# A sample's cached keys: rewritten in memory in blocks of 32, and turned by VectorE instead of TensorE

## The chip, the cores and the metric

The kernel runs on one core of a Trainium2 chip. The metric is the device time of one execution in microseconds; the kernel before took 1939.15 us (median of 3 runs, 1937.5 to 1939.77). The engines of the core work side by side, each in the order of its own instruction list: TensorE (PE: matmuls and transposes by matmul, with its weight loads PEld), VectorE (DVE), ScalarE (ACT), GpSimd (POOL) and SyncE (SP). All DMAs of this kernel are issued from SP's list.

## The reference

One step of a one-layer hybrid trunk, in float32: a normalization, one input projection to 5648 columns, three groups (RG-LRU, dilated-window attention, Mamba-2 SSD), gates, one output projection and a second normalization. There is a prompt of 2048 tokens and there are 8 samples of 4 tokens, each sample with a cache of 1024 positions of keys and values, 8 heads of 64. The change concerns the samples' attention:

```python
DILATIONS = ((128, 1), (512, 4), (2048, 16))

def band_attn_sample(q, k_all, v_all, W, slopes, window, dil):
    span = window // dil
    jd = jnp.arange(span + 1) * dil
    idx = W + jnp.arange(L)[:, None] - jd[None, :]
    ...
    kg = k_all[:, idx]
    vg = v_all[:, idx]
    s = jnp.einsum('blhd,bljhd->blhj', q, kg, preferred_element_type=f32) * (Dh ** -0.5)
    s = s - slopes[:, None] * jd.astype(f32)
    ...
    o = jnp.einsum('blhj,bljhd->blhd', p.astype(vg.dtype), vg, preferred_element_type=f32) / l[..., None]
```

With a cache of 1024 positions the three windows of a sample's 4 tokens reach the last 512 cached positions and, in the first 512, those of the first four residues of every 16: 128 positions. So 640 cached keys of each head are scored.

## The kernel before

The program is written as Python generators that are run in turn; the framework's scheduler then fixes each engine's list and puts in the waits. Where several instructions could go next, the list by and large follows the order in which the program creates them. Each engine, SP too, works through its list strictly in order: an instruction that waits holds all behind it.

**Input projections.** `load_w(c0)` (L140 on) loads a weight tile of 1024x128: SP issues the DMA into `wr` (L143, one buffer), POOL multiplies by the norm's gain (L146), ScalarE makes the rounded part `wh` (L147), VectorE the remainder `wl` (L148); `wh` and `wl` have two buffers each. `project_steps` (L154 on) runs five chunks of tokens over it, each with 8 x 3 matmuls (`mm3`, L82 to L84: `wh` by `xh`, `wh` by `xl`, `wl` by `xh`), then evacuates the chunk and gives one turn to every generator in the list `behind`:

```python
            evac(ps, t0, n)
            for g in behind:
                next(g, None)
            yield
```

The order of the early projections is: values and dt for all tokens (`project_tokens`), then `q_tile(0)`, `q_tile(1)`, `lru_x(0)`, `q_tile(2)`, `ga_tile(0)`, `lru_g(0)`, `lru_x(1)`, `q_tile(3)` and so on. `q_tile`, `ga_tile` and `lru_g` store each evacuated chunk by DMA (`d_q`, `d_ga`, `d_y`). `lru_x(m)` also loads eight small blocks `wab` (L525), and its rest (convolution, gates, then a tail with the scan at L582) runs in turns beside the two projections that follow.

**The samples' attention** (`sample_part`, L887 on) is done for 4 pairs of heads and 2 groups of 4 samples, eight parts in turn, with the steps of seven projections `z_tile` between them. A part loads its keys in two pieces of 2 samples (`kc`, `load_rows`, L879) and one of the far positions (`kf`, `load_far`, L885), turns them by five groups of four TensorE transposes (L903) into PSUM, and copies them into `ktT` (head dimension by 640 positions for 4 samples), with ScalarE and VectorE taking the copies alternately (`evac_copy`). Then come the scores (L924), the softmax on VectorE and ScalarE, six transposes of the weights (L946), the product with the values (L958) and the combination of the two heads.

Of the kernel before, what the change touches and what calls it, by code (L numbers as in the profile page):

```python
# [8 lines left out]
F32 = mybir.dt.float32  # L9
# [23 lines left out]
def tile_hybrid_step(ctx: ExitStack, tc: tile.TileContext, A):  # L33
    nc = tc.nc
    act, dve, pool, pe, sp = nc.scalar, nc.vector, nc.gpsimd, nc.tensor, nc.sync
# [5 lines left out]
    dram = ctx.enter_context(tc.tile_pool(name="dram", bufs=1, space=DRAM))  # L41
# [9 lines left out]
    d_ys = dram.tile([1024, NS], F32, name="d_ys")  # L51
    d_cums = dram.tile([16, NS], F32, name="d_cums")
    d_z = dram.tile([1024, TOK], F32, name="d_z")


    ident = const.tile([128, 128], F32, name="ident")
# [73 lines left out]
    psT = ps_es.enter_context(tc.tile_pool(name="psT", bufs=2, space=PSUM, side="right"))  # L130
# [22 lines left out]
    behind = []  # L153
# [163 lines left out]
    with tc.tile_pool(name="rows", bufs=1) as rp:  # L317
# [10 lines left out]
        tp = psT.tile([128, 4, 128], F32, tag="tp", name="tp")  # L328
# [3 lines left out]
        for g in range(3):  # L332
            tp = psT.tile([128, 4, 128], F32, tag="tp", name="tp")
# [5 lines left out]
        tp = psT.tile([128, 4, 128], F32, tag="tp", name="tp")  # L339
# [6 lines left out]
        dve.tensor_scalar(out=sp8[:, 0], in0=sp8[:, 0], scalar1=-8.0, scalar2=None, op0=OP.mult)  # L346


    def by_residue(ap, np_):

        return ap[:, :np_].rearrange("p (n i r) -> p n r i", r=4, i=32)
# [37 lines left out]
    def k_tile(m):  # L389
        rows = slice(128 * m, 128 * m + 128)  # L390
        k_p = A["k_p"][0, 0].rearrange("t h d -> t (h d)")

        def evac(ps, t0, n):
            np_ = min(n, SEQ - t0)
            kr = p2.tile([128, 512], F32, tag="e", name="kr")
            dve.tensor_copy(out=blocks(kr, np_), in_=by_residue(ps, np_))
            sp.dma_start(out=d_k[rows, t0:t0 + np_], in_=kr[:, :np_])

            ko = p2.tile([128, 512], F32, tag="e", name="ko")
            dve.transpose(out=ko[:, :n], in_=ps[:, :n])  # L400
            for a in range(4):
                pt_, fs = slice(32 * a, 32 * a + 32), slice(128 * m + 32 * a, 128 * m + 32 * a + 32)
                sp.dma_start(out=k_p[t0:t0 + np_, fs].rearrange("(b i) f -> i b f", i=32),
                             in_=ko[pt_, :np_].rearrange("i (b f) -> i b f", f=32))
                if n > np_:
                    sp.dma_start(out=A["k_s"][0].rearrange("b l h d -> (b l) (h d)")[:, fs], in_=ko[pt_, np_:n])
            if n > np_:
                act.copy(out=ksn[:, m], in_=ps[:, np_:n])
        project(C_K + 128 * m, evac)
# [101 lines left out]
    with tc.tile_pool(name="lru", bufs=1) as lp, tc.tile_pool(name="lrus", bufs=2) as ls:  # L511
# [99 lines left out]
        tp = psT.tile([128, 4, 128], F32, tag="tp", name="tp")  # L611
# [6 lines left out]
        sp.dma_start(out=A["lru_h_s"][0], in_=lo[28:36])  # L618

    p2_es.close()  # L620


    z_last = []
# [8 lines left out]
    with tc.tile_pool(name="xbc", bufs=2) as xp, tc.tile_pool(name="xbc1", bufs=1) as xp1:  # L632
        scol = xp1.tile([128, 12, 27], F32, name="scol")
        for m in range(12):
# [4 lines left out]
            for t0, n in CHUNKS:  # L639
                o = xp.tile([128, 512], F32, tag="o", name="o", bufs=3)  # L640
# [3 lines left out]
        for g in range(3):  # L644
            so = xp.tile([27, 512], F32, tag="o", name="so", bufs=3)
            tp = psT.tile([128, 4, 128], F32, tag="tp", name="tp")
# [214 lines left out]
    with tc.tile_pool(name="sa", bufs=1) as sa:  # L861
        evac_n = [0]

        def evac_copy(out, in_):
            evac_n[0] += 1
            if evac_n[0] % 2:
                act.copy(out=out, in_=in_)
            else:
                dve.tensor_copy(out=out, in_=in_)
# [5 lines left out]
        def load_rows(t, cache, pr, bg, b0):  # L875

            rows = cache[0, 4 * bg + b0:4 * bg + b0 + 2].rearrange("b t h d -> b t (h d)")[:, :, 128 * pr:128 * pr + 128]
            for i in range(2):
                sp.dma_start(out=t[:, i], in_=rows[i, 512:1024].rearrange("(j p) c -> p j c", p=128))  # L879

        def load_far(t, cache, pr, bg):

            rows = cache[0, 4 * bg:4 * bg + 4].rearrange("b t h d -> b t (h d)")[:, 0:512, 128 * pr:128 * pr + 128]
            for m in range(4):
                sp.dma_start(out=t[32 * m:32 * m + 32], in_=rows.rearrange("b (g s) c -> s g b c", s=16)[m])  # L885

        def sample_part(pr, bg):  # L887
# [2 lines left out]
            sbias = sa.tile([128, 672], F32, tag="sbias", name="sbias")  # L890
            sp.dma_start(out=sbias, in_=A["c_sbias"][pr, bg])
            ktT = sa.tile([128, 4, 640], F32, tag="ktT", name="ktT")
            for i in range(3):
                if i < 2:
                    kt_ = sa.tile([128, 2, 4, 128], F32, tag="kc", name="kc", bufs=2)
                    load_rows(kt_, A["cache_attn_k"], pr, bg, 2 * i)
                else:
                    kt_ = sa.tile([128, 1, 4, 128], F32, tag="kf", name="kf")
                    load_far(kt_[:, 0], A["cache_attn_k"], pr, bg)
                for h in range(2 if i < 2 else 1):  # L900
                    tp = psT.tile([128, 4, 128], F32, tag="tp", name="tp")
                    for j in range(4):
                        pe.transpose(tp[:, j], kt_[:, h, j], ident)  # L903
                    if i < 2:
                        evac_copy(ktT[:, 2 * i + h, :512], tp.rearrange("p j c -> p (j c)"))
                    else:
                        evac_copy(ktT[:, :, 512:], tp)
                    yield
            for i in range(2):
                load_rows(vt[i], A["cache_attn_v"], pr, bg, 2 * i)  # L910
            load_far(vf, A["cache_attn_v"], pr, bg)
# [3 lines left out]
            for e in range(2):  # L915
                pt_ = slice(64 * e, 64 * e + 64)
                pool.tensor_copy(out=qz[pt_, :, 4 * e:4 * e + 4],
                                 in_=qs[pt_, pr, 16 * bg:16 * bg + 16].rearrange("p (b l) -> p b l", l=NL))
# [8 lines left out]
            p = sa.tile([128, 672], F32, tag="p", name="p")  # L927
# [13 lines left out]
            for g in range(2):  # L941
                tp = psT.tile([128, 4, 128], F32, tag="tp", name="tp")
# [10 lines left out]
            o = psG.tile([128, 512], F32, tag="g", name="so")[:, :128]  # L953
# [10 lines left out]
            tp = psT.tile([128, 4, 128], F32, tag="tp", name="tp")  # L964
# [9 lines left out]
        def fills():  # L974

            parts = [sample_part(pr, bg) for pr in range(4) for bg in range(2)]
            for i, part in enumerate(parts):
                for j in range(6):
                    next(part)
                    yield  # L980
                    if i and j < 4:
                        next(parts[i - 1])
                        yield
            for _ in parts[-1]:
                yield
# [412 lines left out]
    psT = es.enter_context(tc.tile_pool(name="psT2", bufs=1, space=PSUM, side="right"))  # L1398
# [123 lines left out]
    for c in range(16):  # L1522
        k = 0
# [115 lines left out]
```

## Time and profile before

| what | value |
|---|---|
| median of 3 runs | 1939.15 us |
| the profiled execution's own time | 1935.46 us |
| its span | 1933.7 us |
| TensorE busy | 1888.0 us, 98% |
| VectorE, ScalarE, POOL busy | 1075.8, 760.3, 269.4 us |
| mean share of the 16 DMA engines (SP's queue) | 38.7% |

How to read it: the profile is of one execution, and its rows are compared with that execution's own time; the other runs lie up to 4.3 us above it. Busy time is the time in which an engine executes something; matmuls are pipelined, and their ends are modelled, so neighbours overlap and the spacing of their starts tells the cost. Rows of SP (SPq) are the issuing of a DMA, not its transfer. In brackets stands how long the engine was idle ahead of an instruction and which instruction of which engine ended that.

### The profile page before, as it was taken

The numbers are of one execution on the slowest core, as the hardware profiler recorded it, in microseconds if no ns is written. First come the engines' busy times: TensorE is split into PE (matmuls) and PEld (weight loads), VectorE is DVE, ScalarE is ACT, GpSimd is POOL, SyncE is SP. The second block draws the span as 40 slices with busy tenths as digits, with TensorE's granted clock in tenths as the row PEclk, the third lists the DMA queues.
The fourth block names the chain that finished last, engine by engine and source line by source line (L and its number), as shares of the span: only waits on it lengthen the run. The fifth ranks groups of instructions, "written<-read, shape, count | busy, mean of one in ns | idle before, by whom it ended". The sixth has DMA issues, their size and how long they took to land.

```text
span 1933.7 us, 35729 instructions
## 1 busy us (share of the span) xinstructions
PE 1888.0 (98%) x14110; PEld 1552.6 (80%) x14110; DVE 1075.8 (56%) x2354; ACT 760.3 (39%) x1490; POOL 269.4 (14%) x346
## 2 busy tenths in 40 slices
PE   8999999999999999999999999999998999999998
PEld 7998888888888888887877777777766787677876
DVE  7414444454533776664422226666687776667774
ACT  6411636362610222223233436555654333333332
POOL 0100111101010111111000100000023223223231
PEclk9999999999999999998999999999999999999999
DMA  7422121232233222224477753343465444334442
GB/s 235 131 79 74 44 69 47 64 69 63 66 88 79 94 76 74 67 72 138 131 210 205 208 181 115 101 142 102 119 207 161 127 140 124 111 115 130 128 140 66
DMA packets 304500, 222.02 MB, mean 115 GB/s; under 512 B 69171, under 2 KB 260515, under 8 KB 304333
## 3 DMA queue, kind: packets, MB, share of 16 engines
q1 hardware_dynamic: 304332, 219.74, 38.7%
q8 instruction: 111, 1.82, 0.4%
q14 instruction: 57, 0.46, 0.1%
HBM read 150.81 MB, written 68.86 MB: 114 GB/s over the span
## 4 chain that ended last, share of the span: by engine, by line
PE 41%; ACT 4%; DMA 3%; DVE 3%; issue 1%; SPq 1%; POOL 1%; DVEq 0%; ACTq 0%; POOLq 0%
PE ops L83 5%; PE ops L84 5%; PE ops L82 5%; PE mm L82 3%; PE pt L1164 3%; PE mm L84 3%; PE mm L83 3%; PE o L1200 2%; ACT sr L1136 2%; PE s L1109 2%; PE yd L1283 2%; DMA sg<-d_cum 1%; PE yo L1288 1%; PE s L1088 1%; PE stp L1307 1%
## 5 line engine op out<-in xcount | busy, mean ns | idle before, releaser
L82 PE MATMUL mm<-xh,wh 128*128 128x512 f32 (+2 forms) x1600 | 562.4, 351 | 1.8 <-ACT wh L147 0.9
L83 PE MATMUL mm<-xl,wh 128*128 128x512 f32 (+2 forms) x1600 | 561.2, 351 | 0.0
L84 PE MATMUL mm<-xh,wl 128*128 128x512 f32 (+2 forms) x1600 | 559.9, 350 | 0.0
L82 PEld LDWEIGHTS mm<-xh,wh 128*128 128x128 f32 x1600 | 301.5, 188 | 44.4 <-issue 4.3
L84 PEld LDWEIGHTS mm<-xh,wl 128*128 128x128 f32 x1600 | 300.6, 188 | 39.6 <-issue 1.0
L83 PEld LDWEIGHTS mm<-xl,wh 128*128 128x128 f32 x1600 | 301.2, 188 | 37.7 <-issue 0.2
L146 POOL TENSOR_TENSOR wr<-wr,gC 128x1024 f32<-128x1024 f32 x40 | 78.7, 1968 | 407.6 <-DMA wr<-in_w_in_dram 379.5
L436 DVE SCALAR_TENSOR_TENSOR o<-u,ssdc,o 128x512 f32<-128x512 f32 (+2 forms) x216 | 128.6, 618 | 4.8
L1136 ACT ACTIVATE sr<-sr,nm 128x384 f32<-128x384 f32 (+3 forms) x128 | 97.9, 770 | 23.3 <-DVE nm L1132 18.7
L148 DVE SCALAR_TENSOR_TENSOR wl<-wr,wh 128x1024 fp32r<-128x1024 f32 x40 | 48.9, 1223 | 82.9 <-ACT wh L147 82.9
L642 ACT ACTIVATE o<-o 128x512 f32<-128x512 f32 (+2 forms) x60 | 33.1, 552 | 145.7 <-issue 83.2
L1047 ACT COPY ptsb<-pt 128x512 f32<-128x512 f32 x96 | 52.5, 583 | 76.7 <-PE pt L1164 76.6
L720 DVE TENSOR_SCALAR sg<-sg,cum 128x128 f32<-128x128 f32 (+1 forms) x256 | 72.8, 344 | 14.7 <-ACT ecB L718 14.6
L82 PE MATMUL mmt<-wh,xh 128*128 128x256 f32 (+3 forms) x272 | 79.5, 295 | 0.9 <-ACT xh L254 0.6
L84 PE MATMUL mmt<-wh,xl 128*128 128x256 f32 (+3 forms) x272 | 78.6, 290 | 0.0
L83 PE MATMUL mmt<-wl,xh 128*128 128x256 f32 (+3 forms) x272 | 78.1, 288 | 0.0
L434 DVE TENSOR_SCALAR o<-u,ssdc 128x512 f32<-128x512 f32 (+1 forms) x72 | 43.1, 611 | 61.9 <-ACT u L416 60.7
L1164 PE MATMUL pt<-ident,sr 128*128 128x128 f32 x576 | 75.3, 281 | 2.3 <-ACT sr L1136 1.8
L147 ACT ACTIVATE wh<-wr 128x1024 fp32r<-128x1024 f32 x40 | 42.4, 1060 | 87.9 <-PE mm L83 76.9
L1164 PEld LDWEIGHTS pt<-ident,sr 128*128 128x128 f32 x576 | 63.6, 143 | 15.0 <-issue 8.9
L416 ACT COPY u<-mm 128x512 f32<-128x512 f32 (+1 forms) x80 | 39.4, 493 | 91.9 <-PE mm L84 80.2
L718 ACT ACTIVATE ecB<-sg 64x512 f32<-64x512 f32 x60 | 37.8, 630 | 88.3 <-DMA sg<-d_cum 80.5
(520 smaller groups left out, 3551.3 us busy)
## 6 DMA issues: line engine op xcount, KB each, us to landing
wr<-in_w_in_dram SPq DMA_DIRECT2D x40, 512.0 KB
sg<-d_cum SPq DMA_DIRECT2D x30, 512.0 KB
d_xbc<-o SPq DMA_DIRECT2D x36, 256.0 KB
x<-in_x_prompt_dram SPq DMA_DIRECT2D x32, 256.0 KB
kc<-in_cache_attn_k_dram SPq DMA_DIRECT2D x32, 256.0 KB
vt<-in_cache_attn_v_dram SPq DMA_DIRECT2D x32, 256.0 KB
xres<-in_x_prompt_dram SPq DMA_DIRECT2D x32, 256.0 KB
out_dram<-ot SPq DMA_DIRECT2D x32, 256.0 KB
```

Of the source, the lines that this page charges most:

```text
L82: pe.matmul(out, lhsT=wh, rhs=xh, start=start, stop=False)
L83: pe.matmul(out, lhsT=wh, rhs=xl, start=False, stop=False)
L84: pe.matmul(out, lhsT=wl, rhs=xh, start=False, stop=stop)
L146: pool.tensor_tensor(out=wr, in0=wr, in1=gC[:, :, None].to_broadcast([128, 8, 128]), op=OP.mult)
L147: act.activation(out=wh, in_=wr, func=AF.Copy, scale=scale)
L148: dve.scalar_tensor_tensor(out=wl, in0=wr, scalar=scale, in1=wh.bitcast(F32), op0=OP.mult, op1=OP.subtract)
L434: dve.tensor_scalar(out=o, in0=v(0), scalar1=w[:, 0:1], scalar2=b, op0=OP.mult, op1=OP.add)
L436: dve.scalar_tensor_tensor(out=o, in0=v(t), scalar=w[:, t:t + 1], in1=o, op0=OP.mult, op1=OP.add)
L720: dve.tensor_scalar(out=sg[:n, h], in0=sg[:n, h], scalar1=cum[:n, c, 8 * g + h:8 * g + h + 1], scalar2=0.0, op0=OP.subtract, op1=OP.min)
L1047: act.copy(out=out, in_=in_)
L1136: act.activation(out=sr[e][r], in_=sr[e][r], func=AF.Exp, bias=nm[:, e, r:r + 1], accum_out=ll[:, e, r:r + 1])
L1164: pe.transpose(tp[:, r], sr[e][r][:, 128 * g:128 * g + 128], ident)
```

## The change

A tile in memory, `d_kc`, takes the 640 reachable keys of every sample, cut so that each 32x32 block of a position block by head dimension lies where VectorE's transpose of 32x32 blocks needs it. `spread_keys` fills it with DMAs from memory to memory: 8 DMAs for each of 32 blocks, one with 512 pieces of 128 bytes and one with 128 such pieces for each of four samples. The generator `key_blocks` stands in `behind` before `q_tile(0)`, so one block is issued in the program at each of the first 32 projection steps, up to the second of `lru_x(1)`. In `sample_part` four loads of 128x640 take the place of the eight loads of keys, and four `dve.transpose` of 128x640 that of the 20 transposes on TensorE and the five copies from PSUM. `evac_copy` is now called once in a part, for the softmax weights, so ScalarE and VectorE take that copy in turns. All lines behind the new ones move on by one at first and by 18 or 19 later (L147 becomes L148).

```diff
--- before.py
+++ after.py
@@ -51,6 +51,7 @@
     d_ys = dram.tile([1024, NS], F32, name="d_ys")
     d_cums = dram.tile([16, NS], F32, name="d_cums")
     d_z = dram.tile([1024, TOK], F32, name="d_z")
+    d_kc = dram.tile([1024, 4 * 640], F32, name="d_kc")
 
 
     ident = const.tile([128, 128], F32, name="ident")
@@ -346,6 +347,23 @@
         dve.tensor_scalar(out=sp8[:, 0], in0=sp8[:, 0], scalar1=-8.0, scalar2=None, op0=OP.mult)
 
 
+    def spread_keys(pr, bg):
+
+        rows = A["cache_attn_k"][0, 4 * bg:4 * bg + 4].rearrange("b t h d -> b t (h d)")
+        for a in range(4):
+            o = 128 * (2 * pr + bg) + 32 * a
+            fs = slice(128 * pr + 32 * a, 128 * pr + 32 * a + 32)
+            dst = d_kc[o:o + 32].rearrange("k (b t f) -> k b t f", b=4, f=32)
+            for b in range(4):
+                sp.dma_start(out=dst[:, b, :16], in_=rows[b, 512:1024, fs].rearrange("(t k) f -> k t f", k=32))
+
+                sp.dma_start(out=dst[:, b, 16:], in_=rows[b, 0:512, fs].rearrange("(k t) f -> k t f", t=16)[:, :4])
+            yield
+
+    key_blocks = (None for pr in range(4) for bg in range(2) for _ in spread_keys(pr, bg))
+    behind.append(key_blocks)
+
+
     def by_residue(ap, np_):
 
         return ap[:, :np_].rearrange("p (n i r) -> p n r i", r=4, i=32)
@@ -618,6 +636,9 @@
         sp.dma_start(out=A["lru_h_s"][0], in_=lo[28:36])
 
     p2_es.close()
+    behind.remove(key_blocks)
+    for _ in key_blocks:
+        pass
 
 
     z_last = []
@@ -890,22 +911,14 @@
             sbias = sa.tile([128, 672], F32, tag="sbias", name="sbias")
             sp.dma_start(out=sbias, in_=A["c_sbias"][pr, bg])
             ktT = sa.tile([128, 4, 640], F32, tag="ktT", name="ktT")
-            for i in range(3):
-                if i < 2:
-                    kt_ = sa.tile([128, 2, 4, 128], F32, tag="kc", name="kc", bufs=2)
-                    load_rows(kt_, A["cache_attn_k"], pr, bg, 2 * i)
-                else:
-                    kt_ = sa.tile([128, 1, 4, 128], F32, tag="kf", name="kf")
-                    load_far(kt_[:, 0], A["cache_attn_k"], pr, bg)
-                for h in range(2 if i < 2 else 1):
-                    tp = psT.tile([128, 4, 128], F32, tag="tp", name="tp")
-                    for j in range(4):
-                        pe.transpose(tp[:, j], kt_[:, h, j], ident)
-                    if i < 2:
-                        evac_copy(ktT[:, 2 * i + h, :512], tp.rearrange("p j c -> p (j c)"))
-                    else:
-                        evac_copy(ktT[:, :, 512:], tp)
-                    yield
+            kc = []
+            for b in range(4):
+                kc.append(sa.tile([128, 640], F32, tag="kc", name="kc", bufs=4))
+                sp.dma_start(out=kc[b], in_=d_kc[128 * (2 * pr + bg):128 * (2 * pr + bg) + 128, 640 * b:640 * b + 640])
+            for b in range(4):
+                dve.transpose(out=ktT[:, b], in_=kc[b])
+                yield
+            yield
             for i in range(2):
                 load_rows(vt[i], A["cache_attn_v"], pr, bg, 2 * i)
             load_far(vf, A["cache_attn_v"], pr, bg)
```

What this does to the lists of the engines is shown at three places. Numbers behind a name tell one tile from the next. First SP's list around `q_tile(1)`, before: `wr_2359` is the weight of `q_tile(2)`, `q_2068` to `q_2175` are `q_tile(1)`'s chunks but the first, `wab` the small blocks of `lru_x`.

```order
L143 DMA wr_2359<-in_w_in_dram 128x8x128
L525 DMA wab_2938<-in_lru_w_a_dram 64x64 x3
L367 DMA d_q_66<-q_2023 128x512
L525 DMA wab_2938<-in_lru_w_a_dram 64x64
L525 DMA wab_2938<-in_lru_w_x_dram 64x64 x4
L525 DMA wab_3689<-in_lru_w_a_dram 64x64 x4
L525 DMA wab_3689<-in_lru_w_x_dram 64x64
L367 DMA d_q_66<-q_2068 128x512
L525 DMA wab_3689<-in_lru_w_x_dram 64x64 x3
L367 DMA d_q_66<-q_2109 128x512
L495 DMA d_cum_72<-rw_2100 128x2x128
L497 DMA d_cums_74<-rws_1990 16x32
```

And in the changed kernel, from `q_tile(1)`'s last chunk (`q_2248`) on: `wr_2288` is the weight of `lru_x(0)`, the projection that comes next, and `d_kc` are the copies.

```order
L385 DMA d_q_66<-q_2248 128x4x64
L358 DMA d_kc_76<-in_cache_attn_k_dram 32x16x32
L360 DMA d_kc_76<-in_cache_attn_k_dram 32x4x32
L358 DMA d_kc_76<-in_cache_attn_k_dram 32x16x32
L360 DMA d_kc_76<-in_cache_attn_k_dram 32x4x32
L358 DMA d_kc_76<-in_cache_attn_k_dram 32x16x32
L360 DMA d_kc_76<-in_cache_attn_k_dram 32x4x32
L358 DMA d_kc_76<-in_cache_attn_k_dram 32x16x32
L360 DMA d_kc_76<-in_cache_attn_k_dram 32x4x32
L543 DMA wab_2268<-in_lru_w_a_dram 64x64 x4
L543 DMA wab_2268<-in_lru_w_x_dram 64x64 x4
L144 DMA wr_2288<-in_w_in_dram 128x8x128
```

Before, the load for the projection after the next stands ahead of `q_tile(1)`'s stores; now the load for the very next one stands behind its last store, a block of copies and `lru_x(0)`'s eight `wab` loads. The loads of `ga_tile(0)`, `lru_g(0)` and `lru_x(1)` stand likewise behind the last store of the projection ahead of them and a block of copies, that of `lru_x(1)` behind eight `wab` loads too; that of `q_tile(2)` stands behind 40 copies and no store. The first copy of all stands right behind the load of `q_tile(0)`'s weight, among the stores of the value projection.

Second, VectorE's list at the end of `q_tile(2)`, before: `wl_2789` is the weight remainder of the projection after the next, `lru_g(0)`; `xc`, `gi`, `a`, `r` and `sq` belong to `lru_x(0)`'s rest.

```order
L547 TENSOR_TENSOR xc_2347<-xc_2347,gi_2544 128x256
L560 TENSOR_TENSOR xs_2567<-xc_2347,xs_2567 64x288
L148 SCALAR_TENSOR_TENSOR wl_2789<-wr_2786,wh_2788 128x1024
L376 COPY qs_93<-mm_2570 128x32
L547 TENSOR_TENSOR xc_2347<-xc_2347,gi_2599 128x288
L578 TENSOR_TENSOR t8_2666<-a_2646,lruc_1714 128x8
L529 TENSOR_TENSOR wlo_2939<-wab_2938,wg_2949 64x128 x2
```

And in the changed kernel, where `wl_2775` is the remainder for `ga_tile(0)`, the next projection, and L600 is the scan:

```order
L589 SCALAR_TENSOR_TENSOR r_2469<-sq_2830,r_2469 128x288
L598 MEMSET a_2815 128x8
L592 TENSOR_TENSOR r_2469<-r_2469,xc_2468 128x2080
L597 TENSOR_TENSOR r_2469<-r_2469,t8_2835 128x8
L600 SCALAR_TENSOR_TENSOR r_2469<-a_2815,r_2469 128x2080
L149 SCALAR_TENSOR_TENSOR wl_2775<-wr_2772,wh_2774 128x1024
L149 SCALAR_TENSOR_TENSOR wl_2990<-wr_2987,wh_2989 128x1024
L611 TENSOR_TENSOR g_3019<-g_3019,r_2469 128x512
```

The remainder for the next projection has moved behind the whole tail of `lru_x(0)`. On TensorE a transpose of `lcol`, which needs the scan's result, now stands ahead of `ga_tile(0)`'s first matmul, and on ScalarE `q_tile(2)`'s `wh` stands behind the sigmoids of the first gates.

Third, TensorE's list in the first part of the samples' attention, before:

```order
L83 MATMUL mm<-xl_124,wh 128x512
L903 MATMUL tp<-ident,kc 128x128 x4
L84 MATMUL mm<-xh_108,wl 128x512
L82 MATMUL mm<-xh_109,wh 128x512
L903 MATMUL tp<-ident,kc 128x128 x4
L83 MATMUL mm<-xl_125,wh 128x512
L903 MATMUL tp<-ident,kc 128x128 x4
L84 MATMUL mm<-xh_109,wl 128x512
L82 MATMUL mm<-xh_109,wh 128x512
L903 MATMUL tp<-ident,kc 128x128 x4
L83 MATMUL mm<-xl_125,wh 128x512
L84 MATMUL mm<-xh_109,wl 128x512
```

And at the scores of that part in the changed kernel:

```order
L83 MATMUL mm<-xh_112,wh 128x512
L84 MATMUL mm<-xl_128,wh 128x512
L85 MATMUL mm<-xh_112,wl 128x512
L937 MATMUL sc<-ktT,qz 32x512 x4
L937 MATMUL sc<-ktT,qz 32x128 x4
L937 MATMUL sc<-ksn,qz 32x32 x4
L83 MATMUL mm<-xh_105,wh 128x512
L84 MATMUL mm<-xl_121,wh 128x512
```

The groups of four transposes between the projection's matmuls (`mm`) are gone, and the scores of a part follow one another.

## Rows read from the trace of the kernel before

**Rows 1.** The page: span, and the first line of busy times.

```profile
span 1933.7 us, 35729 instructions
PE 1888.0 (98%) x14110; PEld 1552.6 (80%) x14110; DVE 1075.8 (56%) x2354; ACT 760.3 (39%) x1490; POOL 269.4 (14%) x346
```

**Rows 2.** Windows of 100 us: length, each engine busy (x count), PEclk, DMA share, GB/s.

```profile
200.00:300.00 100.00, 99.25 (x542) 86.44 (x541) 46.57 (x68) 47.44 (x73) 10.88 (x11) 1.00 0.18 55
1000.00:1100.00 100.00, 99.06 (x836) 75.31 (x830) 26.72 (x76) 36.80 (x61) 6.73 (x17) 1.00 0.76 210
1100.00:1200.00 100.00, 96.14 (x1275) 74.28 (x1280) 44.48 (x177) 42.03 (x92) 4.32 (x7) 0.98 0.47 140
```

**Rows 3.** Waits of PE, 0 to 1200 us: us in total, times, longest.

```profile
PE mm L82 <- ACT wh L147: 0.9, 1, 0.9
```

**Rows 4.** Timeline of SP's queue: start, us, engine, line, operation, out<-in, count.

```profile
48.16 0.66 SPq L143 DMA_DIRECT2D wr<-in_w_in_dram  x1
159.46 0.54 SPq L143 DMA_DIRECT2D wr<-in_w_in_dram  x1
160.04 1.87 SPq L525 DMA_DIRECT2D wab<-in_lru_w_a_dram  x3
235.80 0.37 SPq L143 DMA_DIRECT2D wr<-in_w_in_dram  x1
```

**Rows 5.** Timeline of SP's queue in k_tile(0): stores in runs of 128 bytes.

```profile
403.07 2.05 SPq L403 DMA_DIRECT2D out_dram<-ko  x4
```

**Rows 6.** Timeline of POOL: the scaling of a weight tile [idle before <-releaser].

```profile
239.78 1.90 POOL L146 TENSOR_TENSOR wr<-wr,gC 128x1024 f32<-128x1024 f32 x1 [25.33 <-DMA wr<-in_w_in_dram]
```

**Rows 7.** Timeline of ACT around q_tile(2): evacuations, weight splits, gates.

```profile
184.84 0.35 ACT L373 COPY q<-mm 128x256 f32<-128x256 f32 x1
206.28 1.06 ACT L147 ACTIVATE wh<-wr 128x1024 fp32r<-128x1024 f32 x1 [2.75 <-PE mm L83]
212.45 1.28 ACT L545 ACT_TABLE_LOAD   x1
213.74 0.68 ACT L545 ACTIVATE r<-gate,lruc 64x512 f32<-64x512 f32 x1
234.42 0.35 ACT L373 COPY q<-mm 128x256 f32<-128x256 f32 x1
240.38 1.28 ACT L383 ACT_TABLE_LOAD   x1
```

**Rows 8.** Timeline of DVE around q_tile(2): weight remainder and scan.

```profile
234.54 1.23 DVE L148 SCALAR_TENSOR_TENSOR wl<-wr,wh 128x1024 fp32r<-128x1024 f32 x1 [1.40 <-ACT wh L147]
253.16 4.49 DVE L582 TENSOR_TENSOR_SCAN r<-a,r 128x2080 f32<-128x2080 f32 x1
```

**Rows 9.** DMA view, 402 to 419.7 us: queue, packets, MB, share.

```profile
q1 hardware_dynamic: 6768, 1.57, 41.8%
```

**Rows 10.** Timeline of PE: one group of a sample's key transposes among projection matmuls.

```profile
977.84 0.39 PE L83 MATMUL mm<-xl,wh 128*128 128x512 f32 x1
978.07 0.60 PE L903 MATMUL tp<-ident,kc 128*128 128x128 f32 x4
978.42 0.48 PE L84 MATMUL mm<-xh,wl 128*128 128x512 f32 x1
978.74 0.39 PE L82 MATMUL mm<-xh,wh 128*128 128x512 f32 x1
```

**Rows 11.** Groups by line, 980 to 1150 us: busy us, mean ns | idle before.

```profile
L903 PE MATMUL tp<-ident,kc 128*128 128x128 f32 x120 | 18.3, 277 | 0.1
```

**Rows 12.** The tile ko: VectorE's transposes, min/median/max ns.

```profile
L400 DVE STREAM_TRANSPOSE ko<-mm x20: 435/704/706, 402.3 to 608.1; 128x512 f32<-128x512 f32 x12, 128x256 f32<-128x256 f32 x4, 128x288 f32<-128x288 f32 x4
```

**Rows 13.** Timeline of PE at a pause before samples().

```profile
892.57 0.64 PE L795 MATMUL tpx<-ident,x 128*96 128x128 f32 x4 [2.20 <-POOL x L708]
```

**Rows 14.** Windows of 5 us after that pause.

```profile
895.00:900.00 5.00, 4.76 (x31) 3.83 (x32) 1.96 (x4) 1.94 (x5) 0.00 (x0) 0.50 0.85 238
900.00:905.00 5.00, 5.00 (x22) 2.62 (x17) 1.80 (x7) 0.47 (x1) 0.00 (x0) 0.62 0.02 3
```


## The prediction

> **What bounds the kernel now.** I read the page first: TensorE is busy for 98% of the span [rows 1]. Then the windows of 100 us, in the two stages that the change touches. In the early projections and in the samples' attention TensorE is busy for 96 to 99 us of every 100, at a granted clock of 0.98 to 1.00, while VectorE has 27 to 47 us of work and the DMA engines stand at a share of 0.18 early and 0.47 to 0.76 later [rows 2]. Third the waits of TensorE: in the first 1200 us it waits for a weight (`wh`) once, for 0.9 us [rows 3]. So the time is TensorE's own work in both stages: work taken from it is saved, and every wait that is new on it is added in full, since nothing behind it is idle enough to give it back. Last I read SP's queue, because all DMAs of this kernel are issued there in one fixed order.
>
> **Part 1, the samples' keys.** 160 transposes go, in 40 groups of four. A group stands between two projection matmuls of 512 columns. Without one between them two matmuls start 0.23 us apart; with one the next starts after 0.58 us and the one behind it after 0.32 instead of 0.23 [rows 10]. That is 0.35 + 0.09 = 0.44 us for a group, and 40 x 0.44 = 17.6 us. By busy time a transpose is 18.3 / 120 = 0.15 us, which makes 24.4 us for 160 [rows 11]; this counts time that overlaps with the neighbours, so I take 17.6 and keep 24.4 as the best case. The worst case is nothing saved, if the scores now wait for VectorE. VectorE gets 32 transposes of 128x640. Its transposes took 704 ns for 512 columns and 435 for 256 [rows 12], 1.05 ns for a column, so 0.84 us for 640 and 27 us in all. It loses 16 copies for them, and it has more than half of each 100 us free there; no cost.
>
> **Part 2, the copies in memory.** 256 DMAs are added, half of them 512 pieces of 128 bytes, half 128 such pieces. No copy from memory to memory is in the trace. The nearest row is the store of the new keys, four DMAs of 512 pieces in 2.05 us on SP's queue, 0.51 us each [rows 5]; I take 0.5 us for every copy, 4.0 us for a block of eight. For the engines: between 402 and 419.7 us twelve such stores and three of 256 KB were 41.8% of 17.7 us, 7.4 us, so at most 0.62 us for 64 KB [rows 9]. 128 large copies and 128 of a quarter make 128 x 0.77 = 99 us at most, beside a share of 0.18, over some 300 us: the first copy stands right behind a weight load that SP issued at 48.16 us [rows 4], the last in lru_x(1), which begins two projections of 22.4 us after q_tile(2)'s end at 234 us [rows 7] and after the waits of part 3, near 353 us. That is hidden, and so is twice that (a copy reads in small pieces too). From below it costs nothing; from above I bound it with four times the stores' price, see the third rival.
>
> The Trainium skill ("DMA: Bandwidth & Descriptors", Specifications) says that a transfer below 512 bytes misses line rate, because it is done as read-modify-write. The stores above are such transfers and their price holds that already; if the rule made a copy twice as dear, the sum would be the same.
>
> **Part 3, what the copies stand in front of.** This is the term that decides. The order written by the scheduler follows the program, and a weight load comes in the program after the copies of all earlier steps. Before, SP issues the load for q_tile(2) at 159.46 us, before the first store of q_tile(1) [rows 4]. In the changed order the load for lru_x(0) stands behind the last store of q_tile(1), one block of copies and eight loads of `wab`; that store waits for ScalarE's evacuation of the last chunk, so SP cannot reach the load before TensorE has finished q_tile(1) and has nothing to multiply. The same pattern, read off the order: ga_tile(0) behind the last store of q_tile(2), lru_g(0) behind that of ga_tile(0), lru_x(1) behind that of lru_g(0). A load late by this path costs: 3.98 us from issue to POOL's start (235.80 to 239.78) [rows 4, 6], POOL 1.90 [rows 6], ScalarE's `wh` 1.06 [rows 7], VectorE's `wl` 1.23 [rows 8] less two matmuls of 0.23 that go ahead: 7.7 us together. The evacuation takes 0.35 [rows 7] and the store's own issue about what a load's does, 0.4; eight `wab` loads at 1.87 / 3 are 5.0 us [rows 4].
>
> - q_tile(1) to lru_x(0): 0.35 + 0.4 + 4.0 + 5.0 + 7.7 = 17.5 us.
> - lru_x(0) to q_tile(2): no store is between, and 40 copies (20 us) and the path stay beside the projection's matmuls (24 for each 512 columns of 2080 at 0.23 us, 22.4 us, and the wait of 7.7 us ahead of them), so the load is in time. But the gates of chunk 0 and their sigmoids now stand ahead of `wh` on ScalarE: 0.35 + 1.28 + 4 x 0.68 + 1.06 + 0.8 less four gate matmuls of 0.23 is 5.3 us [rows 7].
> - q_tile(2) to ga_tile(0): the load would be there after 12.5 us, but VectorE's `wl`, and a transpose of `lcol` on TensorE, now stand behind the scan of lru_x(0)'s tail. Before, from the evacuation at 234.42 to the scan's end at 253.16 + 4.49 were 23.2 us [rows 7, 8], in which ScalarE also worked for ga_tile(0) (a table load of 1.28 [rows 7] and a few pieces of half a microsecond); that, some 3 us, now comes later. 23.2 - 3 + 0.8 = 21.0 us.
> - ga_tile(0) to lru_g(0): 0.35 + 0.4 + 4.0 + 7.7 = 12.5 us.
> - lru_g(0) to lru_x(1): `wab` again, 17.5 us.
>
> Together 73.8 us. After that 16 copies are left, the loads run two projections ahead again, and all is as before. A pause also costs clock. After a wait of 2.20 us at 892 us [rows 13] the granted clock was 0.50 and 0.62 in the next two windows of 5 us [rows 14], that is 1.2 GHz for most of them, a loss of up to 2.5 + 1.9 = 4.4 us. For the four long waits I take 2.5 us each, 10 us, bounds 0 and 18.
>
> **Sum.** 73.8 + 10 - 17.6 = +66 us. The profiled execution took 1935.5 us (1.8 us of it outside the span of 1933.7 [rows 1]), so 2001.7; the median of the runs, 1939.15, lies 3.7 us above it: 2005 us.
>
> **Rivals.**
> - *Faster.* The waits are short and the saving stays: 1939.2 - 17.6 = 1921.5 us. For it: TensorE is bound by work in both stages and SP is idle for most of a projection. It decides from the point where the five waits together are under 17.6 us, 3.5 us each; against it, the path from a late load alone is 7.7 us, and four loads stand behind a store that ends after the projection.
> - *Waits of two thirds.* The loads land earlier beside little traffic, some of the `wab` loads are quicker, the clock costs nothing, and the saving is the larger one: 50 - 24.4 = +26, 1965 us. For it: each price above is that of a queue with other work in it. At a fifth of the waits this becomes no change.
> - *Slow copies.* Reading 128-byte pieces from memory and writing them there costs four times the stores' price: 128 x 3.1 = 397 us of engines from about 50 us on, so the last copy ends near 445 us instead of some 360 (that is 353 and the last blocks), and the weight loads behind it with it: 85 us more, 2090 us. For it: no row shows such a copy. Against it: stores of the same pieces kept SP's pace of 0.51 us with no wait. The skill's rule named above would speak for it if it held for both sides of a copy.
> - *The blocks don't do what they say.* Copies that were not done when the samples' keys are wanted, at 978 us [rows 10], would hold the scores; they end 600 us earlier, so I give this nothing.
>
> **How the numbers follow.** The forecast has 0.74, two thirds of the waits 0.09, slow copies 0.08, faster 0.07, no change 0.02. A measurement of this kernel can tell 0.2%, 4 us, from no change. Slower is 0.91, same 0.02, faster 0.07. The range of 8 in 10 goes from 1962 (waits of two thirds) to 2060 (waits a third longer, clock at 18 us, half of the slow case); 2005 lies in it by the sum.
>
> **What would show it.** In the profile after: TensorE's waits for `wh` (line 148 there) or for the transposes of `lcol` in the stretch from 150 to 400 us, 12 to 22 us long and four of them, one of about 5; 32 VectorE transposes of 0.8 us; the copies' issues near 0.5 us; the stage of the samples' attention some 18 us shorter, with TensorE still at 96 to 99%. Wrong would be: a TensorE at 99% through the projections, or copies whose issues take several us each, or a sample stage that did not shrink.

## The result and the profile after

The changed kernel takes 2011.36 us (median of 3 runs, 2009.39 to 2016.06) against 1939.15 us: ratio 1.0391, 95% interval 1.0373 to 1.041. It is slower by 72 us where 66 were forecast. The profiled execution took 2011.36 us, 75.9 us more than the one of before.

First the page of the changed kernel (span, busy times, the granted clock in 40 slices of 50 us). TensorE is busy for 12 us less than before [rows 1], in a span 76 us longer, so its share has fallen from 98 to 93%; the clock row dips in one place only, from 150 to 400 us.

```profile
span 2009.6 us, 35550 instructions
PE 1875.6 (93%) x13950; PEld 1543.3 (77%) x13950; DVE 1085.3 (54%) x2366; ACT 748.2 (37%) x1469; POOL 269.2 (13%) x346
...
PEclk9998877799999999999999999999999999999999
```

The windows of 100 us (length, busy time of each engine, granted clock, DMA share, GB/s) answer to [rows 2]. From 200 to 400 us TensorE is busy for 68 and 59 of 100 us instead of 99; the DMA engines are far from full there. The samples' stage is as tight as before.

```profile
200.00:300.00 100.00, 67.91 (x307) 56.04 (x308) 36.67 (x53) 39.93 (x58) 7.80 (x10) 0.79 0.34 65
300.00:400.00 100.00, 58.67 (x283) 49.06 (x282) 15.67 (x22) 11.62 (x20) 6.00 (x4) 0.78 0.35 72
...
1100.00:1200.00 100.00, 99.07 (x864) 78.67 (x864) 39.93 (x99) 36.61 (x60) 9.53 (x18) 1.00 0.77 234
```

The five pauses on TensorE's timeline (start, length of the instruction, and in brackets the idle time before it and what ended it); before, the only wait for `wh` up to 1200 us was one of 0.9 us [rows 3]. They are the five of part 3, in its order, 88.2 us together:

```profile
204.29 0.80 PE L83 MATMUL mm<-xh,wh 128*128 128x512 f32 x1 [19.98 <-ACT wh L148]
...
235.66 0.79 PE L83 MATMUL mm<-xh,wh 128*128 128x512 f32 x1 [4.79 <-ACT wh L148]
...
287.21 0.40 PE L631 MATMUL tp<-ident,lcol 128*36 128x128 f32 x1 [22.20 <-POOL lcol L602]
...
330.50 0.79 PE L83 MATMUL mm<-xh,wh 128*128 128x512 f32 x1 [18.26 <-ACT wh L148]
...
379.22 0.79 PE L83 MATMUL mm<-xh,wh 128*128 128x512 f32 x1 [23.00 <-ACT wh L148]
```

On SP's queue the first of them is read off directly, in contrast to [rows 4], where even the load of q_tile(2), one projection further on, stood ahead of q_tile(1)'s stores. TensorE is done with q_tile(1) at 204.29 - 19.98 = 184.31; its last store goes at 186.16, then eight copies, then `wab`, then the load, and 7.16 us after the load's issue TensorE starts.

```profile
186.16 0.54 SPq L385 DMA_DIRECT2D d_q<-q  x1
186.74 0.56 SPq L358 DMA_DIRECT2D d_kc<-in_cache_attn_k_dram  x1
187.34 0.63 SPq L360 DMA_DIRECT2D d_kc<-in_cache_attn_k_dram  x1
...
191.29 0.63 SPq L360 DMA_DIRECT2D d_kc<-in_cache_attn_k_dram  x1
191.96 2.52 SPq L543 DMA_DIRECT2D wab<-in_lru_w_a_dram  x4
194.52 2.51 SPq L543 DMA_DIRECT2D wab<-in_lru_w_x_dram  x4
197.13 0.53 SPq L144 DMA_DIRECT2D wr<-in_w_in_dram  x1
```

To split the sum I took three instructions that both kernels have. VectorE's copy `lo<-tp`, which ends the lru part, starts at 711.8 us instead of 608.5: the early stage costs 103.3 us, 88.2 of it in the five pauses, and 15.1 remain, most of it clock (below). The load of `smask` at the head of the samples' stage goes at 1076.1 instead of 973.3 us, and the last `zo` behind that stage is written at 1232.8 instead of 1154.4: 156.7 us instead of 181.1, so 24.4 us are saved there. The other 3 us are differences of half a microsecond ahead of that stage and 2.5 behind it, which nothing in the change explains. 88.2 + 15.1 - 24.4 - 3 = 75.9.

The tile `ktT` in the view of one line: 32 transposes by VectorE, min/median/max in ns, first and last start.

```profile
L919 DVE STREAM_TRANSPOSE ktT<-kc x32: 801/840/848, 1082.0 to 1184.9; 128x640 f32<-128x640 f32 x32
```

### The profile page after: what moved, and what is told of

It reads as the page before. It is cut to its first block, busy times and chain, and to the rows that moved or that the text cites. A ratio compares the mean times of both kernels' runs of the same rounds, so it can differ in the third digit from the quotient of the medians.

```text
span 2009.6 us, 35550 instructions
## 1 busy us (share of the span) xinstructions
PE 1875.6 (93%) x13950; PEld 1543.3 (77%) x13950; DVE 1085.3 (54%) x2366; ACT 748.2 (37%) x1469; POOL 269.2 (13%) x346
## 5 line engine op out<-in xcount | busy, mean ns | idle before, releaser
L147 POOL TENSOR_TENSOR wr<-wr,gC 128x1024 f32<-128x1024 f32 x40 | 79.6, 1989 | 481.0 <-DMA wr<-in_w_in_dram 460.7
L148 ACT ACTIVATE wh<-wr 128x1024 fp32r<-128x1024 f32 x40 | 42.4, 1060 | 93.2 <-PE mm L84 57.5
L1126 DVE CUSTOM_DVE_ANT_0 sr<-s,bias 128x128 f32<-128x128 f32 (+3 forms) x128 | 58.7, 486 | 23.1 <-PE s L1122 22.1
```

What stands on the lines that cost most here:

```text
L147: pool.tensor_tensor(out=wr, in0=wr, in1=gC[:, :, None].to_broadcast([128, 8, 128]), op=OP.mult)
L1126: dve.tensor_tensor_reduce(out=sr[e][r][:, :nk], in0=ps[e][:, :nk], in1=bs[:, e, 512 - nk:512], scale=1.0, scalar=NEG, op0=OP.add, op1=OP. ...
```

## The experiments

The theory to test: the loss is one of order. The weight loads stand behind the copies on SP's one queue, and what TensorE loses is fixed by these places. The main rival (A): the loss is that of moving 10 MB in pieces of 128 bytes, wherever the copies stand. All ratios are to the kernel before, run on the same chip; its medians were 1935 to 1937 us beside runs 1 to 9 and 1939 us beside the changed kernel.

| kernel | median us | ratio, 95% interval |
|---|---|---|
| changed kernel | 2011.36 | 1.0391 (1.0373 to 1.041) |
| 1 copies only | 2035.99 | 1.0522 (1.0503 to 1.0541) |
| 2 transposes by VectorE only | 1913.2 | 0.9884 (0.9867 to 0.9902) |
| 3 two copies per step | 1912.33 | 0.9885 (0.9869 to 0.9902) |
| 4 loads a projection earlier | 1958.17 | 1.0118 (1.0103 to 1.0133) |
| 5 two copies per step, keys the old way | 1935.07 | 0.9995 (0.9986 to 1.0005) |
| 6 small copies, keys the old way | 2028.06 | 1.0482 (1.0464 to 1.05) |
| 7 four copies per step | 1955.46 | 1.0095 (1.0079 to 1.0112) |
| 8 sixteen copies per step | 2019.2 | 1.0432 (1.0416 to 1.0447) |
| 9 eight copies at every fourth step | 1912.47 | 0.9878 (0.986 to 0.9896) |

**1, the copies alone.** The changed kernel with the samples' part of the kernel before (its `load_rows`, `load_far`, transposes and `evac_copy`).

> The copies are made as in the changed kernel, but the samples' keys go the old way (160 transposes by TensorE); the copied block is written and not read. In the changed kernel the last transposes of lcol came 103 us later than before, and the samples' stage then took 24 us less. Order theory (weight loads stand behind the copies on SP's queue): 1939 + 103 = about 2042 us, with TensorE's waits of 80 to 95 us between 180 and 400 us in the same five places. Rival A (the price is that of moving the data, not of the order) expects the same here. A rival in which the new transposes or the loads of their tiles cost something in the late stages would give 2010 or less here.

Measured 2036 us, 100 us over before, with the same five waits, each within 1.4 us of the changed kernel's (the fifth wait for `wh` in this list is a later one of 0.4 us):

```profile
PE mm L83 <- ACT wh L148: 65.2, 5, 23.2
PE tp L631 <- POOL lcol L602: 22.4, 1, 22.4
```

So the whole loss is made by the copies, in the early stage.

**2, VectorE's transposes alone.**

```diff
-    behind.append(key_blocks)
-    sp.dma_start(out=kc[b], in_=d_kc[128 * (2 * pr + bg):..., 640 * b:640 * b + 640])
+    keys = A["cache_attn_k"].rearrange("o b t h d -> (o b t h d)")[:1024 * 2560].rearrange("(p f) -> p f", f=2560)
+    sp.dma_start(out=kc[b], in_=keys[128 * (2 * pr + bg):..., 640 * b:640 * b + 640])
```

> No copies; VectorE transposes the same number of tiles of the same shape, loaded straight from the key cache as it lies in memory, so the samples' scores are made from other keys than the reference's. Order theory: no waits of TensorE for wh in the early projections, TensorE at 99 of 100 us from 100 to 400 us as before, the samples' stage 24 us shorter: 1939 - 24 = 1915 us. My forecast's term for the transposes, 17.6 us, would give 1921.5. A rival in which the stage got shorter only because it stood at another place beside other work would give 1930 to 1939.

Measured 1913.2 us, 23 us under before. Together with run 1 the two halves of the change add up: +100 - 23 = +77 against +72 to +76.

**3, the same copies, two after each step.**

```diff
             for b in range(4):
                 sp.dma_start(out=dst[:, b, :16], ...)
                 sp.dma_start(out=dst[:, b, 16:], ...)
-            yield
+                yield
...
-    behind.remove(key_blocks)            # behind p2
+    behind.remove(key_blocks)            # behind the xbc projections
```

> The same 256 copies, two after each step of a projection instead of eight, so that they last into the later projections; the samples' keys as in the changed kernel. In its order on SP every weight load stands at least one whole projection before the projection that uses it. Order theory: no long wait for wh (under 10 us in all between 100 and 700 us), the saving of the samples' stage stays: 1915 us, 1912 to 1925. Rival A (moving 128-byte pieces through memory costs by itself, by DMA engines or memory being busy): the same copies cost the same, 1990 to 2015 us.

Measured 1912.3 us. All 256 copies are made, from 49 to 483 us, and TensorE does not wait for `wh` between 100 and 600 us. The windows show more DMA traffic than in the changed kernel between 200 and 400 us (share 0.38 and 0.37 against 0.34 and 0.35), with TensorE at 99:

```profile
200.00:300.00 100.00, 99.25 (x537) 86.17 (x536) 46.16 (x67) 47.39 (x73) 11.06 (x11) 1.00 0.38 85
300.00:400.00 100.00, 99.25 (x533) 86.04 (x532) 45.67 (x68) 48.79 (x76) 11.73 (x12) 1.00 0.37 84
```

SP's queue in this kernel, loads and last stores only. The load at 161.13 is q_tile(2)'s and the one at 187.80, after the last store of q_tile(1), is ga_tile(0)'s: each stands two projections ahead of its use.

```profile
161.13 0.53 SPq L144 DMA_DIRECT2D wr<-in_w_in_dram  x1
...
186.80 0.37 SPq L385 DMA_DIRECT2D d_q<-q  x1
187.80 0.38 SPq L144 DMA_DIRECT2D wr<-in_w_in_dram  x1
...
210.22 0.38 SPq L144 DMA_DIRECT2D wr<-in_w_in_dram  x1
```

That speaks against rival A: the same copies, beside more traffic in all, and no loss. The copies alone are somewhat less dense here than in the changed kernel, some 140 against 170 between 200 and 400 us; run 6 settles what their data cost. It is also a version that beats both kernels, the one before by 1.2%.

**4, the loads moved ahead instead of the copies.** A table `follows` gives the projection that comes next; its weights are loaded and split after the first step of the one before it.

```diff
-        wh, wl = load_w(c0, scale)
+        wh, wl = ready.pop(c0, None) or load_w(c0, scale)
...
             evac(ps, t0, n)
+            if c0 in follows:
+                c1, s1 = follows.pop(c0)
+                ready[c1] = load_w(c1, s1)
             for g in behind:
```

> The same 256 copies in blocks of eight after each step, as in the changed kernel, but the program loads and splits the weights of the next projection after the first step of the projection before it, ahead of that step's copies. On SP every load then stands about a projection ahead of its use, behind at most the stores of the projection before. Order theory: the waits for wh between 180 and 400 us fall from 88 us to under 10, and the time is 1915 us, 1912 to 1925. Rival A: 1990 to 2015 us, since copies are as many, as dense and at the same place. Rival B (the splitting of weights on POOL, ScalarE and VectorE was what came late, through the scan and the gates ahead of it): also near 1915 here, but then the two-per-step kernel would keep most of its waits.

Measured 1958 us: half the loss gone, not all of it, so my 1915 was wrong. The waits for weights and `lcol`, 88 us in the changed kernel, are 28 here, and 6 more at the gates' weights (`wg`). The largest that is left is ga_tile(0)'s. Three views of it, POOL, ScalarE and TensorE: the load was issued at 225.65 and POOL had scaled the weight at 230.55 + 2.44 = 232.99, but `wh` stands on ScalarE behind the tail of lru_x(0) and starts at 255.38.

```profile
230.55 2.44 POOL L147 TENSOR_TENSOR wr<-wr,gC 128x1024 f32<-128x1024 f32 x1 [20.34 <-DVE xc L576]
...
253.53 1.94 ACT L602 ACTIVATE r<-r 128x2080 f32<-128x2080 f32 x1
255.38 1.04 ACT L148 ACTIVATE wh<-wr 128x1024 fp32r<-128x1024 f32 x1
...
256.47 0.79 PE L83 MATMUL mm<-xh,wh 128*128 128x512 f32 x1 [14.75 <-ACT wh L148]
```

So rival B holds a part: a load that is one projection ahead is not enough where the split of the weight then stands behind gates and a tail. Loads two projections ahead in blocks of eight were not run, so how much of the rest is rival B's is open.

**5, do copies so spread cost anything?** Run 3's copies with run 1's samples' part.

> Two copies after each step as in the two-per-step kernel, but the samples' keys go the old way (160 transposes by TensorE; the copied block is written and not read). Order theory: copies so spread cost nothing at all, 1936 us (1932 to 1941), the same as the kernel before; the whole gain of the two-per-step kernel, 24 us, is then that of the samples' keys. Rival C (the spread copies cost some 10 us that the larger gain hides, or the spread order saves some): 1946 or 1926.

Measured 1935.07 against 1935.14 us, ratio 0.9995 (0.9986 to 1.0005): they cost nothing. The transposes are then worth 1935.1 - 1912.3 = 23 us, the same as in run 2 (runs 3 and 5 are of two chips, on which the kernel before differs by 1 us).

**6, a sixteenth of the data in the same places.**

```diff
-sp.dma_start(out=dst[:, b, :16], in_=rows[b, 512:1024, fs].rearrange("(t k) f -> k t f", k=32))
+sp.dma_start(out=dst[:2, b, :16], in_=rows[b, 512:1024, fs].rearrange("(t k) f -> k t f", k=32)[:2])
```

(and `[:2]` likewise in the copy of the far keys, `16:`).

> As the kernel with the copies only (eight after each step, the samples' keys the old way), but each copy moves a sixteenth of its data (32 pieces of 128 bytes, or 8); number, places and order on SP are the same row for row, and the copied block is not read. Order theory: the price is that of the places and of the issues. If an issue still takes 0.6 us, about 2036 us as with the full copies; if it falls to the 0.25 to 0.3 us of the small loads of lr, a block is 2.6 us shorter and four waits with it: 2026. Rival A (the price is that of the data): 100 / 16, so about 1942 us.

Measured 2028 us. Of the 100 us, 93 stay with a sixteenth of the bytes; the DMA share between 200 and 300 us is 0.10, and the five pauses are there (18.05, 4.79, 22.88, 16.13, 20.52 us, 82.4 together):

```profile
PE mm L83 <- ACT wh L148: 59.5, 4, 20.5
PE tp L631 <- POOL lcol L602: 22.9, 1, 22.9
```

That excludes rival A: the price is that of the places. An issue takes 568 ns here, against 599 and 627 in the changed kernel, so it hardly depends on the size. For issues of that length I had expected 2036 us; of the 8 us less, 5 lie in the pauses, and the others I have not traced. The rule weighed in the prediction (the Trainium skill, "DMA: Bandwidth & Descriptors", Specifications, on transfers below 512 bytes) can have no more than these 8 us, and in run 3 none of the time.

**7 and 8, other rates.** In `spread_keys` the `yield` stands behind every second `b` (four copies per step) or behind every second `a` (sixteen). In run 7, as in runs 3 and 9, the generator stays in `behind` through the xbc projections.

> Four copies after each step, samples' keys as in the changed kernel. In its order on SP one load alone stands behind the last store of the projection before its own, that of lru_x(2) behind lru_g(1)'s, with one load of wab between; all others stand about a projection ahead. Order theory: one wait of 9 us there, perhaps 5 more where the split of a weight stands behind gates or a tail, 2 to 4 us of clock: 1920 to 1930 us. Rival D (the cost grows evenly with the copies of a step, between 1912 for two and 2010 for eight): 1945.

> Sixteen copies after each step, so that all 256 are done in three and a bit projections; samples' keys as in the changed kernel. In its order on SP three loads are late: q_tile(1) behind the last store of q_tile(0) and 16 copies, lru_x(0) behind the last store of q_tile(1), 16 copies and wab, q_tile(2) behind 80 more copies. Order theory with 0.65 us for a copy: 0.75 + 10.4 + 7.7 = 19 us, 24 us, and 52 + 7.7 less the 30 us from the load of lru_x(0) to its end, 30 us; 73 us in three waits at three places, up to 20 more at ga_tile(0) behind the tail, clock 10: 1912 + 83 to 103 = 1995 to 2015 us. Rival D (evenly with the copies of a step): over 2100 us. Rival A (the data alone): 2010 with no such places.

Four per step took 1955 us, 25 over what I expected, and is nearer to rival D's 1945. The wait at lru_x(2) is there (10.46 us, 9 expected), but I had overlooked the load of ga_tile(2), which stands behind the last store of k_tile(0) and so meets lru_x(2)'s tail, just as ga_tile(0) does in the changed kernel:

```profile
390.25 0.79 PE L83 MATMUL mm<-xh,wh 128*128 128x512 f32 x1 [10.46 <-ACT wh L148]
...
463.38 0.40 PE L632 MATMUL tp<-ident,lcol 128*36 128x128 f32 x1 [21.22 <-POOL lcol L603]
```

The place was in the order and the reading was mine, so the run speaks for places rather than for an even growth. On the queue these copies are as spread as run 3's, from 49 to 477 us, and two loads are late all the same, behind the last store of the projection ahead of their own. Run 8 settles the even growth. Sixteen took 2019 us, not over 2100, with three waits in the three places named, of 27.0, 43.5 and 27.8 us (19, 24 and 30 expected). The second shows what my formula lacked. TensorE finished q_tile(1) at 256.97 - 43.46 = 213.51, but SP issued that projection's last store only at 233.64, because 16 copies take 10.5 us and a step 5.5: SP was 20 us behind before the store came. From the store on, the terms hold: 11.1 us with its 16 copies, 5.2 of `wab`, 7.1 of load and split.

```profile
233.64 0.54 SPq L386 DMA_DIRECT2D d_q<-q  x1
...
244.70 2.52 SPq L544 DMA_DIRECT2D wab<-in_lru_w_a_dram  x4
247.26 2.51 SPq L544 DMA_DIRECT2D wab<-in_lru_w_x_dram  x4
249.88 0.53 SPq L144 DMA_DIRECT2D wr<-in_w_in_dram  x1
```

**9, rate or block?** Blocks of eight, with three empty steps behind each (`for _ in range(4): yield`).

> Blocks of eight copies as in the changed kernel, but one block after every fourth step of a projection only: the same rate as two per step, in the same bursts as the changed kernel. Order theory: the order on SP has every weight load at least half a projection ahead, no long wait, 1912 us (1907 to 1918). Rival E (the size of the block that stands together in the program is what decides, not the rate): 1950 us or more.

Measured 1912.5 us, as with two per step. The order written for SP is nearly that of run 3: the scheduler spreads a block over the steps that follow it. So the rate in the program decides whether the loads come ahead, not the size of a block, and not the density on the queue either, which in run 7 is that of run 3.

## Why the prediction was right, step by step

**Part 3, the five waits.** Place, order and releaser came as forecast; the sum was 14.4 us short.

| wait | forecast | measured |
|---|---|---|
| q_tile(1) to lru_x(0) | 17.5 | 19.98 |
| lru_x(0) to q_tile(2) | 5.3 | 4.79 |
| q_tile(2) to ga_tile(0) | 21.0 | 22.20 |
| ga_tile(0) to lru_g(0) | 12.5 | 18.26 |
| lru_g(0) to lru_x(1) | 17.5 | 23.00 |

Two terms were mis-sized. The first is "I take 0.5 us for every copy, 4.0 us for a block of eight", from [rows 5]: a copy takes 0.60 or 0.63 us and a gap of 0.04, a block 5.2 to 5.5 (186.74 to 191.96), and three of the waits have one: 3.9 us. The second is the larger: "The evacuation takes 0.35 and the store's own issue [...] 0.4". The copies behind the last store do not begin 0.75 us after TensorE's end, since the block of the step before still stands ahead of that store. For ga_tile(0) TensorE ended at 330.50 - 18.26 = 312.24 us, in the midst of that block, and SP reached the store at 317.20:

```profile
311.34 0.54 SPq L385 DMA_DIRECT2D d_ga<-ga  x1
311.92 0.56 SPq L358 DMA_DIRECT2D d_kc<-in_cache_attn_k_dram  x1
...
316.47 0.63 SPq L360 DMA_DIRECT2D d_kc<-in_cache_attn_k_dram  x1
317.20 0.54 SPq L385 DMA_DIRECT2D d_ga<-ga  x1
317.79 0.56 SPq L358 DMA_DIRECT2D d_kc<-in_cache_attn_k_dram  x1
...
322.56 0.62 SPq L360 DMA_DIRECT2D d_kc<-in_cache_attn_k_dram  x1
323.28 0.54 SPq L144 DMA_DIRECT2D wr<-in_w_in_dram  x1
```

The last two steps of a projection have 256 and 288 columns, about half a step of work each, and a block outlasts them. From TensorE's end to the first copy behind the store pass 2.4, 5.6 and 5.4 us in the three waits, 11.1 more than forecast. I had taken SP as free whenever the store became ready, though 40 copies at my own price were 20 of a projection's 22.4 us. The late path from the load's issue (7.7 in the sum, 7.2 measured to TensorE's start) and `wab` (5.0 and 5.2) held: 1.5 us less over three waits, and 0.3 more over two. The short wait came out right with some luck. I had the load of q_tile(2) in time by 2.4 us; at the true price of 40 copies it went at 224.37, POOL had the weight scaled only at 232.77, and the sigmoids, which end at 234.53, decide the wait by 1.8 us:

```profile
230.83 1.94 POOL L147 TENSOR_TENSOR wr<-wr,gC 128x1024 f32<-128x1024 f32 x1
...
234.56 1.06 ACT L148 ACTIVATE wh<-wr 128x1024 fp32r<-128x1024 f32 x1
```

**The clock.** Forecast 10 us, bounds 0 and 18; the 103.3 us of the early stage leave 15.1. After each of the five pauses, the short one too, the granted clock is 0.50, the lower level of 1.2 GHz, in the next window of 5 us:

```profile
204.00:209.00 5.00, 4.67 (x10) 3.28 (x11) 1.23 (x1) 0.23 (x1) 0.00 (x0) 0.50 0.40 63
235.00:240.00 5.00, 4.29 (x9) 2.98 (x10) 1.48 (x2) 0.61 (x1) 0.00 (x0) 0.50 0.00 0
287.00:292.00 5.00, 4.79 (x12) 3.83 (x13) 0.00 (x0) 0.00 (x0) 0.34 (x4) 0.50 0.00 0
330.00:335.00 5.00, 4.46 (x10) 3.07 (x11) 1.23 (x1) 0.45 (x1) 0.00 (x0) 0.50 0.22 36
379.00:384.00 5.00, 4.74 (x10) 3.31 (x11) 1.22 (x1) 0.17 (x1) 0.00 (x0) 0.50 0.41 64
```

On TensorE's timeline after the first pause matmuls start 0.43 us apart until 209.98 and 0.23 apart from 210.37 on:

```profile
208.70 0.63 PE L83 MATMUL mm<-xh,wh 128*128 128x512 f32 x1
209.13 0.63 PE L84 MATMUL mm<-xl,wh 128*128 128x512 f32 x1
...
210.37 0.39 PE L84 MATMUL mm<-xl,wh 128*128 128x512 f32 x1
210.60 0.39 PE L85 MATMUL mm<-xh,wl 128*128 128x512 f32 x1
```

The 13 matmuls from 204.29 on take 6.1 us until 210.37, and at 0.23 us apart they would take 3.0, so this pause costs 3.1 us more than its wait. The same count behind the others gives 2.8, 2.4, 3.1 and 2.7 us: 14.1 of the 15.1. In all but the third some 0.4 us of it passes at the third matmul, which waits for `wl`; the sum has that in its path. A pause's clock was thus well sized at 2.5 us (2.3 to 2.7), but I had counted four.

**Part 1, the transposes.** Forecast 17.6 us, best case 24.4; the stage gave 24.4, and runs 2 and 5 gave 23. That the best case came out is luck in part, since the busy time of a group, 0.61 us [rows 11], is not its price. Added up by the spacing of TensorE's starts in that stage of both kernels, the transposes give 19.0 us, the projections' matmuls 2.5, and the scores, which now follow one another, about 3. The group that I read closely [rows 10] was a cheap one, with 0.35 us to the next start; ahead of the scores and the values it is 0.52 to 0.59:

```profile
985.55 0.66 PE L903 MATMUL tp<-ident,kf 128*128 128x128 f32 x4
986.14 1.06 PE L924 MATMUL sc<-ktT,qz 128*32 128x512 f32 x6
```

My sum did not have the 3 us of the scores, and why they got cheaper is not shown. VectorE's 0.84 us per transpose is the measured median, and no wait of TensorE in that stage is longer than 0.6 us.

**Part 2, the copies.** That the copies as such are hidden is shown by run 5 at two per step, and by run 6, where a sixteenth of their data leaves 93 of the 100 us. That twice their price would be hidden too was not run. The issue's price was read off stores and was too low, as above.

**The sum.** Short by 14.4 us in the waits and 5.1 in the clock, short by 6.8 in the saving, and 3 us of a later stage: 9.7 us between 66 and 75.9 on the profiled executions. Right in its mechanism, and in its size partly because errors of both signs met. Of the rivals, "waits of two thirds" (88 us measured, 50 there), "slow copies" (issues of 0.6 us, the last copy at 382 us) and "faster" are excluded; "faster" is what the same copies give at a lower rate.

## What to carry to other kernels

A DMA that costs nothing in bytes still takes a place in its queue: ask of each one that is added which load stands behind it in the order, and whether that load is still a full stage ahead of its use. Compare the queue's issue time per step with the step itself, the shortest steps above all; as they come near each other, prefetching stops with no engine and no memory full. Here two copies per step (1.3 us of issue for a step of 5.5) left every load in time; four (2.6 us) put two loads behind the last store of the projection ahead of their own, and eight (5.2 us) four of them. When a transfer has hundreds of microseconds to spare, give it out at the lowest rate that still ends in time.

## What the runs showed of the hardware that was not expected

The issue of a copy from memory to memory on SP's queue hardly depends on its size: 599 ns for 512 pieces of 128 bytes, 627 for 128 of them, 568 for 32 or 8 (medians of 128 each). A pause of 4.79 us cost as much in clock, some 2.4 us, as pauses of 18 to 23 us, 2.3 to 2.7.
